# A transformer block on one core: gated channels tile by tile, keys' splits on VectorE, nearer deadlines in the planner

## The chip, the core and the metric

One core of a Trainium2 chip runs the whole kernel. The engines are TensorE (PE; its weight loads are listed as PEld), VectorE (DVE), ScalarE (ACT), GpSimd (POOL) and SyncE (SP, which issues the DMAs). The metric is the device time of one execution in microseconds (us); lower is better. Beside it stands a profile of one execution, with a time for each instruction.

## What is computed

One layer with batch 1, 1024 tokens, model width 1024 and 256 memory tokens, all in float32, in three residual sub-layers:

```python
h = rms_norm(x, pre_mix_g)
z = h @ w_in + b_in                         # 1024 x 1792
z_a, z_b, z_c = z[:, :256], z[:, 256:1024], z[:, 1024:]
y_a = pool_mixer(z_a, pool_w, pool_scale)   # trailing means over 2, 4, 8, 16 tokens, per-group linear
y_b = spatial_gating_mixer(z_b, ...)        # gelu, layer norm, 128x128 causal token mix, gate
y_c = conformer_conv_mixer(z_c, ...)        # a*sigmoid(g), 31-tap causal conv, layer norm, swish
x = x + rms_norm(concat([y_a, y_b, y_c]) @ w_out, post_mix_g)

h = rms_norm(x, pre_x_g); m = rms_norm(mem, mem_g)
x = x + rms_norm(cross_attention(h, m, wq, wk, wv, wo), post_x_g)   # 4 heads of 256

h = rms_norm(x, pre_ff_g)
x = x + rms_norm(square(relu(h @ w_ff1)) @ w_ff2, post_ff_g)        # width 4096
```

The part `z_c` is 768 wide: 384 values `a` and 384 gates `g`. The 384 gated channels are three tiles of 128.

## The kernel before

**Products.** Each float32 operand is split into a high part (`hi`, a rounded copy, made by ScalarE) and a low part (`lo`, the source less the high part, made by `lo_of` on VectorE or GpSimd). `mm3` (line 445) then makes three matmuls: hi x hi, hi x lo, lo x hi. The large square products (`om`, the mixer's output projection; `pq`, the queries; `ox`, the attention's output projection; and both MLP products `fx`, `fz`, `fy` and `g`) are made by `seven` and like helpers, with seven half-size products in place of eight and sums of operands on VectorE.

**Order by a planner.** The program is not issued as it is written. `Schedule.record` (line 148) notes every operation with its engine, its modelled cost (`_cost`, line 204), what it depends on, and its place in the record. `order` (line 231) then plans up to six times: each pass takes TensorE's order from the pass before (the first pass takes that of the record), and the pass with the shortest modelled span is issued. In `_order` (line 249) an operation gets a due time. It starts as TensorE's modelled time at that place of the record plus `SLACK`, 50000 ns, and is then lowered by those who use its result, down to the TensorE instruction that needs it:

```python
                due[i] = at + self.SLACK
...
                due[i] = min(due[i], due[u] - o.cost - self.LAT[op.eng][o.eng])
```

The planner places, again and again, the operation that can start first; among operations of an engine that can start at the same time, the nearer due time wins (on TensorE, the earlier place in the record). A PSUM bank (eight of 128x512, line 423) or a slot in SBUF is given when its first user is placed, as long as tiles recorded earlier can still get theirs. Each engine then runs its instructions in the order so found. A load on SP waits until TensorE has issued what was recorded 150 TensorE instructions before it.

**The first stage, up to `om`.** `norm_in` (line 558) normalises the tokens of one half (512 tokens, four blocks of 128), transposes them and leaves `h1[hf][k]` with both parts. The loop at line 602 makes the gated channels: for tile `j` and token half `hf`, 24 matmuls for the gates (`zg`), 24 for the values (`za`), a sigmoid on ScalarE (`sg`), and on VectorE the gated product into `hc[j]`, stored as even and odd tokens, and their sum into `hs[j]`. Its order is (0,0), (1,0), (0,1), (1,1), (2,0), (2,1). Within the first turn the second half of the tokens is normalised and tile 1's weights are loaded and split:

```python
            W("zc1")
            norm_in(1, [0, 1, 2, 3])
```

`conv_taps(j)` (line 644) needs all tokens of tile `j`: 47 scaled additions on VectorE in three sums, each in a PSUM bank (`cacca`, `caccb`, `caccc`), then the sum into `cs`. `conv_norm(hf, cs)` (line 666) transposes blocks of 128 tokens (`cnat`), takes mean and variance on VectorE, the reciprocal root on GpSimd (`rstd_of`, line 454: names ending in `e` are the request, in `r` the root), normalises on VectorE (`cn`), transposes back (`cback`) and applies gain, bias and swish (`csg`). It is recorded behind the keys but with a lead of 300 places (lines 869 to 872).

Beside this run the other mixers (`zb`, `sv`, `ybt`; pooling adds `zw` on GpSimd and `zp` on VectorE, line 727), the memory's normalisation (`memt`, `mT`) and the keys: `mem_product("wk")` (line 839) holds four PSUM banks (`wkp`) and takes 12 matmuls for each of eight rows of weights `wk0` to `wk7`; its result is copied (`kn`) and transposed (`kt`, `kT`). The rows of weights come from `row_unit` (line 504): a load of 128x1024, the high part on ScalarE, the low part either as one VectorE subtraction or as two GpSimd ones of 128x512. Line 519 chooses: rows of `w_in` (`ZR`) and of the keys (`WK`) on GpSimd, rows of the values (`WV`) on VectorE.

`om` starts with its first product, from channels 0 to 511 of the first half (`oma10`, `oma11`) and the first quarter of `w_out` (`omww10`, `omww11`); the convolution's channels come in with its second. Behind it follow the values (`wvp`), `pq`, attention, `ox` and the MLP.

Of the kernel before, what the change touches and what calls it, by code (L numbers as in the profile page):

```python
# [20 lines left out]
NK = D // P  # L21
# [44 lines left out]
class Schedule:  # L66
# [12 lines left out]
           "pe": {"act": 197, "dve": 196, "pe": 0, "pool": 200, "sync": 100},  # L79
           "pool": {"act": 75, "dve": 60, "pe": 309, "pool": 102, "sync": 100},  # L80
           "sync": {"act": 2100, "dve": 2100, "pe": 2100, "pool": 2100, "sync": 2100}}
    SLACK = 50000.0
    PASSES = 6
    BYDUE = ("act", "dve", "pool", "sync")
    TABLE = {AF.Sigmoid: "sigmoid", AF.Gelu_apprx_tanh: "gelu", AF.Exp: "exp"}
# [117 lines left out]
    @staticmethod  # L203
    def _cost(eng, method, args, kw, ins):
        n = 1
        for d in args[0].shape[1:]:
            n *= d
        if method == "dma_start":
            return max(450.0, n * args[0].shape[0] * 4 / 240.0)
        size = lambda a: int(np.prod(a.shape[1:]))  # L210
        if eng == "pe":
            passes = 4 if method == "matmul" and args[1].dtype == F32 else 1
            return max(109.0, 13.4 + passes * n * 0.4167)
        wide = [a for a in ins if size(a) > 1]
        ptrs = len(ins) - len(wide) if n > 1 else 0
        if eng == "act":
            c = 51.0 + 0.833 * n + (0.0 if ins[0].space == bass.MemoryType.PSUM else 42.0)
            return c + 93.0 * min(ptrs, 1) + (93.0 if "accum_out" in kw else 0.0)
        if eng == "pool":
            if method == "tensor_tensor":  # L220
                return 520.0 if n < 17 else 60 + 2.4 * n
            return 60 + 1.0 * n
        n = max([n] + [size(a) for a in wide])
        psum = any(a.space == bass.MemoryType.PSUM for a in ins + [args[0]])
        if not psum and len(wide) == 1 and method in ("tensor_scalar", "tensor_scalar_mul",
                                                      "tensor_copy"):
            return 69 + 0.52 * n + 61.0 * ptrs
        return 69 + 1.042 * n + 61.0 * ptrs
# [20 lines left out]
    def _order(self, pe_order):  # L249
# [18 lines left out]
        for i, op in enumerate(ops):  # L268
            if op.eng == "pe":
                at = max(at, due[i])  # L270
            else:
                due[i] = at + self.SLACK
        for i in range(len(ops) - 1, -1, -1):
# [129 lines left out]
def block_kernel(ctx: ExitStack, tc: tile.TileContext, x, mem, pre_mix_g, w_in, b_in, pool_w,  # L403
# [5 lines left out]
    act, dve, pool, pe, sync = sc.act, sc.dve, sc.pool, sc.pe, sc.sync  # L409
# [10 lines left out]
    def slot(name, shape, dt=F32):  # L420
        return sc.slot(name, shape, dt)

    def bank(name):
        return sc.tile(pp, [P, 512], F32, "b", 8, name)
# [91 lines left out]
            return hi, lo  # L516
        return go

    ZR, WK, WV = [pool] * NK, [pool] * NK, [dve] * NK
    units, made = {}, {}  # L520
    for j in range(3):
        units[f"zc{j}"] = col_unit(f"zc{j}", [(w_in, 1024 + j * P), (w_in, 1408 + j * P)], j == 0)
# [7 lines left out]
    def W(name):  # L530
        if name not in made:
            made[name] = units[name]()
        return made[name]
# [5 lines left out]
    def columns(name, vecs):  # L539

        rows = slot(name + "r", [P])
        at, res = 0, []
        n_all = sum(n for _, n in vecs)
        cols = sc.tile(cp, [P, n_all], F32, name, 1, name)
        for v, n in vecs:
            src = v if v.shape[0] == n else v.rearrange("o (r p) -> (o r) p", p=P)
            sync.dma_start(rows[at:at + n, :], src)
            res.append(cols[:, at:at + n])
            at += n
        ps = bank(name + "p")  # L550
        pe.transpose(ps[:, :n_all], rows[:n_all, :], ident[:n_all, :n_all])
        dve.tensor_copy(cols, ps[:, :n_all])
        return res
# [4 lines left out]
    def norm_in(hf, blocks):  # L558

        if h1[hf] is None:  # L560
            h1[hf] = [slot(f"h1_{hf}_{k}", [2, H], F32R) for k in range(NK)]
        nb = len(blocks)
        xs, ms = [], small(f"p0ms{hf}{blocks[0]}", 4)
        for b in blocks:
            bb = hf * 4 + b
            xt = slot(f"x{bb}", [D])
            sync.dma_start(xt, x[bb * P:(bb + 1) * P, :])
            act.activation(junk, xt, AF.Square, scale=1.0 / 32, accum_out=ms[:, b:b + 1])
            r = rstd_of(f"p0{bb}", ms[:, b:b + 1], 1)
            dve.tensor_scalar_mul(xt, xt, r)  # L570
            xs.append(xt)
        if not g:
            g.append(columns("gmix", [(pre_mix_g, 8)])[0])
            W("zc0")
        per = 4 // nb
        c = slice(blocks[0] * P, (blocks[-1] + 1) * P)
        for k0 in range(0, NK, per):
            bk = bank(f"p0t{hf}{blocks[0]}{k0}")
            for k in range(k0, k0 + per):
                ps = bk[:, (k - k0) * nb * P:(k - k0 + 1) * nb * P]  # L580
                for i in range(nb):
                    pe.transpose(ps[:, i * P:(i + 1) * P], xs[i][:, k * P:(k + 1) * P], ident)
            for k in range(k0, k0 + per):
                ps = bk[:, (k - k0) * nb * P:(k - k0 + 1) * nb * P]
                act.activation(h1[hf][k][:, 0, c], ps, AF.Identity, scale=g[0][:, k:k + 1])
                dve.scalar_tensor_tensor(h1[hf][k][:, 1, c], ps, g[0][:, k:k + 1],
                                         h1[hf][k][:, 0, c].bitcast(F32), ALU.mult, ALU.subtract)
# [5 lines left out]
    def prod_t(ps, w, a, b, act_h, c0=0, c1=H):  # L593
        for k in range(NK):
            mm3(ps[:, c0:c1], w[0](k, a, b), w[1](k, a, b), act_h[k][:, 0, c0:c1],
                act_h[k][:, 1, c0:c1], k == 0, k == NK - 1)
# [2 lines left out]

    hc = [slot(f"hc{j}", [2, H]) for j in range(3)]  # L600
    hs = [slot(f"hs{j}", [H]) for j in range(3)]
    for j, hf in ((0, 0), (1, 0), (0, 1), (1, 1), (2, 0), (2, 1)):
        w = W(f"zc{j}")
        pa, pg = bank(f"za{j}{hf}"), bank(f"zg{j}{hf}")
        if (j, hf) == (0, 0):
            for q in range(2):
                if q:
                    norm_in(0, [2, 3])
                prod_t(pg, w, 128, 256, h1[hf], q * 256, q * 256 + 256)
                prod_t(pa, w, 0, 128, h1[hf], q * 256, q * 256 + 256)  # L610
            W("zc1")
            norm_in(1, [0, 1, 2, 3])
            (g_x, g_ff, g_mem, bA, bC, pscale, cb, clg, clb, sgb) = columns("vec", [
                (pre_x_g, 8), (pre_ff_g, 8), (mem_g, 8), (b_in[:, 0:256], 2), (b_in[:, 1024:1792], 6),
                (pool_scale, 2), (conv_b, 3), (conv_ln_g, 3), (conv_ln_b, 3), (sg_b[0], 4)])
            cw = columns("taps", [(conv_w[0].rearrange("k (j p) -> (k j) p", p=P), 93)])[0].rearrange(
                "p (k j) -> p k j", j=3)
        else:
            prod_t(pg, w, 128, 256, h1[hf])
            prod_t(pa, w, 0, 128, h1[hf])  # L620
        sg = slot(f"sg{j}{hf}", [H])
        act.activation(sg, pg, AF.Sigmoid, bias=bC[:, 3 + j:4 + j])
        c = slice(hf * 256, hf * 256 + 256)
        dve.scalar_tensor_tensor(hc[j][:, :, c], pa.rearrange("p (n t) -> p t n", t=2),
                                 bC[:, j:j + 1], sg.rearrange("p (n t) -> p t n", t=2),
                                 ALU.add, ALU.mult)
        dve.tensor_tensor(hs[j][:, c], hc[j][:, 0, c], hc[j][:, 1, c], ALU.add)
# [703 lines left out]
    for ch in range(2):  # L1331
# [17 lines left out]
        for i, g, first in ((1, 0, True), (2, 1, True), (6, 0, False), (5, 1, True), (7, 0, False),  # L1349
# [22 lines left out]
            n = 1 if ch == 1 and i == 4 else 3  # L1372
# [60 lines left out]
```

## Time and profile before

| | |
|---|---|
| median of 3 runs | 1169.54 us (1169.51 to 1169.66) |
| the profiled execution | 1169.37 us |
| its span, first to last instruction | 1167.7 us |
| TensorE busy | 1142.2 us (98%) |
| VectorE busy | 917.0 us (79%) |
| ScalarE busy | 570.9 us (49%) |
| GpSimd busy | 168.2 us (14%) |
| granted TensorE clock, mean | 0.995 of full |

In all views times are us from the start of the span. Busy time of TensorE is modelled at its end, since matmuls overlap: a matmul of 512 columns is listed with some 390 ns and yet one follows the other every 227 ns. Nearly all rows have the line L162, where the planner's record calls the engine, so groups are told apart by the tiles' names: out<-in, buffer numbers partly left out. An idle time in brackets is followed by what ended it.

### The profile page before, as it was taken

The page shows a single profiled execution, that of the slowest core. Times are in us where ns is not written, and L with a number is a line of the kernel's source. Part 1 is how long each engine was busy: PE and PEld are TensorE (multiplying, and loading weights), DVE is VectorE, ACT ScalarE, POOL GpSimd, SP SyncE. Part 2 cuts the span into 40 slices and gives each one's busy share as a digit, 9 for nine tenths or more (in the row PEclk, how much of TensorE's full clock was granted, in tenths as well). Part 3 has the DMA queues.
Part 4 walks back from the last instruction along what each step waited for, and adds up shares of the span by engine and source line. Part 5 has one row for each costly group of instructions (what it writes and reads, how often), then busy time and mean ns, then how long its engine had stood idle before and what let it go on. Part 6 is the DMA issues. An engine that isn't in the chain of part 4 may idle for free.

```text
span 1167.7 us, 14569 instructions
## 1 busy us (share of the span) xinstructions
PE 1142.2 (98%) x5319; PEld 948.6 (81%) x5319; DVE 917.0 (79%) x1278; ACT 570.9 (49%) x998; POOL 168.2 (14%) x194
## 2 busy tenths in 40 slices
PE   7999999799999999999999999999999999999997
PEld 6788877688887898888888888888888888888885
DVE  5499999898988769988999777567679744487736
ACT  6332145666984368749843343334446433435321
POOL 4360229301347000013000000000000000000001
PEclk9999999899999999999999999999999999999999
DMA  7400025114761222236045535443775444443443
GB/s 263 146 30 1 1 89 207 47 62 150 256 253 55 90 72 91 73 119 225 17 136 210 186 137 184 158 146 116 241 263 189 162 163 155 153 160 116 174 144 145
DMA packets 87078, 163.11 MB, mean 140 GB/s; under 512 B 6474, under 2 KB 29918, under 8 KB 87006
## 3 DMA queue, kind: packets, MB, share of 16 engines
q1 hardware_dynamic: 87006, 162.17, 39.8%
q8 instruction: 42, 0.69, 0.2%
q14 instruction: 30, 0.25, 0.1%
HBM read 116.01 MB, written 46.14 MB: 139 GB/s over the span
## 4 chain that ended last, share of the span: by engine, by line
PE 87%; DVE 7%; ACT 4%; issue 1%; POOL 0%; DMA 0%; POOLq 0%; DVEq 0%; ACTq 0%
PE g L162 25%; PE fx L162 13%; PE fz L162 7%; PE om L162 7%; PE pq L162 6%; PE ox L162 5%; PE zb L162 4%; PE fy L162 3%; PE zg L162 3%; PE za L162 3%; PE sc L162 2%; PE o L162 2%; PE wvp L162 2%; PE wkp L162 2%; DVE caccc L162 1%; ACT oxh L162 1%
## 5 line engine op out<-in xcount | busy, mean ns | idle before, releaser
L162 POOL TENSOR_TENSOR fr0r<-fr0e,half 128x1 f32<-128x1 f32 x1 | 0.9, 863 | 581.9 <-DVE fr0e L162 581.9
L162 ACT COPY c<-fx 128x512 f32<-128x512 f32 x48 | 29.0, 603 | 87.8 <-PE fx L162 84.6
L162 DVE TENSOR_TENSOR acc<-acc,g 128x512 f32<-128x512 f32 x40 | 26.9, 684 | 46.1 <-PE g L162 46.1
L162 DVE TENSOR_TENSOR c<-c,fz 128x512 f32<-128x512 f32 x32 | 22.0, 687 | 16.5 <-ACT c L162 16.5
L162 DVE SCALAR_TENSOR_TENSOR c<-c 128x512 f32<-128x512 f32 x48 | 33.3, 693 | 0.7
L162 DVE SCALAR_TENSOR_TENSOR caccc<-hs,cws,caccc 128x511 f32<-128x511 f32 (+14 forms) x45 | 33.5, 744 | 0.2
L162 DVE SCALAR_TENSOR_TENSOR cacca<-hc,taps,cacca 128x511 f32<-128x511 f32 (+14 forms) x45 | 32.2, 746 | 0.0
L162 ACT ACTIVATE junk<-acc 128x512 f32<-128x512 f32 x16 | 10.2, 635 | 44.7 <-DVE acc L162 42.7
L162 DVE TENSOR_TENSOR w1o<-w1a,w1o 128x512 fp32r<-128x512 f32 x32 | 21.6, 689 | 12.6 <-ACT w1o L162 12.6
L162 DVE SCALAR_TENSOR_TENSOR caccb<-hc,taps,caccb 128x511 f32<-128x511 f32 (+13 forms) x42 | 30.5, 745 | 0.0
L162 PE MATMUL sc<-kv,q 128*128 128x256 f32 x192 | 27.5, 288 | 0.0
L162 ACT CAST w1o<-w1a 128x512 fp32r<-128x512 f32 x32 | 19.6, 640 | 14.7 <-DVE sb L162 6.2
L162 PEld LDWEIGHTS sc<-kv,q 128*128 128x128 f32 x192 | 24.9, 190 | 0.7
L162 DVE TENSOR_TENSOR sa<-c 128x512 f32<-128x512 f32 x16 | 11.1, 695 | 18.0 <-ACT c L162 16.5
L162 ACT ACTIVATE c<-fx 128x512 f32<-128x512 f32 x16 | 9.6, 598 | 31.6 <-PE fx L162 31.6
L162 PE MATMUL o<-pT,kv 128*128 128x512 f32 x96 | 24.4, 393 | 0.0
L162 ACT CAST w1o<-w1c 128x512 fp32r<-128x512 f32 x32 | 19.5, 624 | 6.9 <-PE fx L162 4.1
L162 PE MATMUL fx<-h3a10h,w1o 128*128 128x512 f32 x64 | 22.7, 392 | 0.0
L162 DVE TENSOR_TENSOR w1o<-w1c,w1o 128x512 fp32r<-128x512 f32 x32 | 21.6, 689 | 1.2 <-ACT w1o L162 1.2
L162 PE MATMUL fx<-h3a60h,w1o 128*128 128x512 f32 x64 | 22.5, 389 | 0.0
L162 PE MATMUL fx<-h3a11h,w1o 128*128 128x512 f32 x64 | 22.3, 389 | 0.0
L162 PE MATMUL fx<-h3a70h,w1o 128*128 128x512 f32 x64 | 22.3, 389 | 0.0
(1656 smaller groups left out, 4116.8 us busy)
## 6 DMA issues: line engine op xcount, KB each, us to landing
ha<-scr_hid SPq DMA_DIRECT2D x56, 512.0 KB
scr_hid<-c SPq DMA_DIRECT2D x48, 256.0 KB
scr_hid<-sa SPq DMA_DIRECT2D x32, 256.0 KB
scr_hid<-sb SPq DMA_DIRECT2D x32, 256.0 KB
x<-in_x_dram SPq DMA_DIRECT2D x8, 512.0 KB
omwb<-in_w_out_dram SPq DMA_DIRECT2D x8, 512.0 KB
omx<-in_x_dram SPq DMA_DIRECT2D x8, 512.0 KB
scr_x<-omx SPq DMA_DIRECT2D x8, 512.0 KB
```

The costliest lines, as they stand in the source:

```text
L162: op.fn = lambda: f(*[put(a) for a in args], **{k: put(v) for k, v in kw.items()})
```

## The change

Four edits. `SLACK` goes from 50000 to 20000 ns, so that work whose result TensorE does not need soon falls due 30 us earlier. The modelled rate of a DMA goes from 240 to 270 bytes per ns, in the planner only. The low parts of the keys' weights are made by VectorE, one subtraction of 128x1024 for each of the eight rows, instead of by GpSimd in two halves. And the gated channels are recorded with both token halves of tile 0 first, then both of tile 1, then both of tile 2; where weights are fetched and the second half of the tokens is normalised is recorded as before.

```diff
-    SLACK = 50000.0
+    SLACK = 20000.0
...
-            return max(450.0, n * args[0].shape[0] * 4 / 240.0)
+            return max(450.0, n * args[0].shape[0] * 4 / 270.0)
...
-    ZR, WK, WV = [pool] * NK, [pool] * NK, [dve] * NK
+    ZR, WK, WV = [pool] * NK, [dve] * NK, [dve] * NK
...
-    for j, hf in ((0, 0), (1, 0), (0, 1), (1, 1), (2, 0), (2, 1)):
+    for j, hf in ((0, 0), (0, 1), (1, 0), (1, 1), (2, 0), (2, 1)):
         w = W(f"zc{j}")
```

## Rows read from the trace of the kernel before

**Rows 1.** The page's first part: busy time (share of the span) and instructions.

```profile
span 1167.7 us, 14569 instructions
...
PE 1142.2 (98%) x5319; PEld 948.6 (81%) x5319; DVE 917.0 (79%) x1278; ACT 570.9 (49%) x998; POOL 168.2 (14%) x194
```

**Rows 2.** Busy time by stretch, later stages. Columns: stretch, its us, engines, clock, DMA.

```profile
313.00:337.00 24.00, 24.00 (x124) 20.28 (x123) 22.32 (x25) 18.72 (x52) 9.35 (x8) 1.00 0.74 257
...
545.00:582.00 37.00, 36.83 (x178) 30.08 (x176) 36.14 (x45) 32.92 (x73) 5.92 (x6) 1.00 0.19 66
...
860.00:1150.00 290.00, 290.00 (x1281) 240.23 (x1280) 191.05 (x196) 116.21 (x140) 4.03 (x5) 1.00 0.46 161
```

**Rows 3.** The same view, first stage up to the output projection.

```profile
44.00:55.00 11.00, 11.00 (x50) 9.13 (x49) 1.94 (x4) 1.62 (x2) 2.52 (x2) 1.00 0.16 49
...
98.00:140.00 42.00, 41.44 (x192) 34.09 (x191) 41.94 (x82) 10.31 (x23) 6.69 (x9) 1.00 0.00 1
...
140.00:190.00 50.00, 48.49 (x230) 38.81 (x229) 48.63 (x95) 22.68 (x39) 21.69 (x25) 1.00 0.35 122
...
200.00:219.00 19.00, 18.57 (x93) 14.44 (x93) 16.02 (x26) 6.99 (x11) 12.18 (x11) 1.00 0.38 139
...
219.00:232.00 13.00, 7.51 (x38) 5.49 (x37) 10.96 (x24) 12.63 (x24) 3.69 (x4) 0.74 0.00 1
```

**Rows 4.** Timeline of TensorE: start us, us, what, xcount, [idle before <-releaser].

```profile
18.04 1.91 PE L162 MATMUL p0t<-ident,x 128*128 128x128 f32 x16
...
31.71 0.73 PE L162 MATMUL zg<-h,zc1h 128*128 128x512 f32 x2
...
43.25 0.61 PE L162 MATMUL zg<-h,zc0h 128*128 128x512 f32 x2
...
191.57 0.49 PE L162 MATMUL cnat<-ident,cs 128*128 128x128 f32 x3
...
219.02 0.60 PE L162 MATMUL cback<-ident,cn 128*128 128x128 f32 x4
...
231.36 0.69 PE L162 MATMUL om<-omww10h,oma10h 128*128 128x512 f32 x1
```

**Rows 5.** Timeline of VectorE, same columns.

```profile
29.59 5.36 DVE L162 SCALAR_TENSOR_TENSOR h<-p0t,gmix,h 128x512 fp32r<-128x512 f32 x8 [1.14 <-ACT h L162]
...
55.53 0.75 DVE L162 TENSOR_SCALAR cacca<-hc,taps 128x512 f32<-128x512 f32 x1
...
57.49 0.75 DVE L162 TENSOR_SCALAR caccc<-hs,cws 128x512 f32<-128x512 f32 x1
...
188.36 0.74 DVE L162 SCALAR_TENSOR_TENSOR cs<-caccc,cb,cua 128x512 f32<-128x512 f32 x1
...
213.45 1.22 DVE L162 TENSOR_TENSOR oma11l<-yq,oma11h 128x1024 fp32r<-128x1024 f32 x1
...
214.58 0.67 DVE L162 TENSOR_SCALAR cn<-cnat,cmv,cr00r 128x384 f32<-128x384 f32 x1
```

**Rows 6.** Timelines of VectorE, then GpSimd: the root's request, a split, the root.

```profile
193.23 0.15 DVE L162 TENSOR_SCALAR cr00e<-cmv 128x1 f32<-128x1 f32 x1
...
204.23 3.41 POOL L162 TENSOR_TENSOR wk7l<-wk7r,wk7h 128x512 fp32r<-128x512 f32 x2
...
207.60 0.99 POOL L162 TENSOR_TENSOR cr00r<-cr00e,half 128x1 f32<-128x1 f32 x1
```

**Rows 7.** Groups by line and shape, VectorE, 44:232 (xcount | busy us, mean ns | idle).

```profile
L162 DVE SCALAR_TENSOR_TENSOR zp<-zw,zaT 64x512 f32<-64x512 f32 x4 | 6.1, 1532 | 0.1
...
L162 DVE SCALAR_TENSOR_TENSOR zp<-zw,zaT 64x496 f32<-64x496 f32 x4 | 2.7, 667 | 0.1
...
L162 DVE TENSOR_TENSOR oma10l<-yq,oma10h 128x1024 fp32r<-128x1024 f32 x1 | 2.4, 2355 | 0.0
...
L162 DVE TENSOR_TENSOR omww10l<-omwb,omww10h 128x1024 fp32r<-128x1024 f32 x1 | 1.2, 1226 | 0.0
```

**Rows 8.** Waits of TensorE, whole span (us in total, times, longest).

```profile
PE pq L162 <- DVE h2a61l L162: 0.9, 1, 0.9
```

## The prediction

> **What bounds the kernel now.** I read the page first: TensorE works 1142.2 of 1167.7 us [rows 1]. The change removes no TensorE work, so what it can win is TensorE's lost time. I then cut the span into stretches. From 860 us on nothing is lost: TensorE is busy 290 of 290 us with VectorE at 191 [rows 2]. In 313:337 and 545:582 TensorE is also full, but VectorE is nearly so (22.32 of 24, 36.14 of 37): places where order can hurt. The large loss lies just ahead of the output projection of the mixer. In 219:232 TensorE works 7.51 of 13 us and its granted clock averages 0.74 [rows 3]; the clock fell behind idle time, toward the lower of its two levels (1.2 of 2.4 GHz), and so stretches the work that is left.
>
> The size of that hole: from the transpose at 219.02 to the first `om` matmul at 231.36 are 12.3 us [rows 4]. Of the 38 instructions in 219:232 [rows 3], three are matmuls and 35 are transposes. Sixteen transposes in a row took 1.91 us with the last one's end, so one costs about 0.11 us and 35 cost 3.8. **The hole is 8.5 us**; the stretch before it, 200:219, loses 0.4.
>
> Why it is there: `om`'s first product was not late. Its last operand, `oma11l`, is written at 213.45, for 1.22 us [rows 5]. What is left for the end is the normalisation of the convolution (`cnat`, `cback`) and `kt`. The first `cnat` comes at 191.57 [rows 4], after the last convolution sum at 188.36 [rows 5]; but the reciprocal root of its variance, asked for by VectorE at 193.23, is made by GpSimd only at 207.60 [rows 6]. GpSimd's queue was in the keys' weight splits, 3.4 us for the last of eight alone [rows 6]. For 14 us each `cnat` keeps its PSUM bank, beside the four banks of the keys' product, out of eight. The whole normalisation is so pushed behind that product, and at the end runs as a bare chain ScalarE, VectorE, TensorE.
>
> **The order of channels.** It moves 48 matmuls and their sigmoid and products; DMAs are recorded where they were. Before, tile 1's first half runs from 31.71 to 43.25 and tile 0's second half follows [rows 4]; the first tap is at 55.53 [rows 5]. After, tile 0 is whole when TensorE reaches 43.25, and taps start about 10.5 us sooner. VectorE worked only 1.94 of the 11 us in 44:55 [rows 3], so **9.1 us of idle VectorE time are filled**. From 98 to 190 it is full (41.94 of 42, 48.63 of 50), so this moves its whole queue forward. What it costs on TensorE: tile 0's second half needs the second token half normalised, which tile 1's first half did not. VectorE writes those eight `h` low parts from 29.59 over 5.36 us [rows 5], so the last is there at 34.95; TensorE, starting at 31.71 and using at least three matmuls of 0.23 us for each, wants the last at 36.5. I take 0; if it waited for all of them, +3.2; if weights of tile 1 that come late stop mattering, -0.5. On the queues, tile 1's splits (GpSimd) and loads (SP) only gain 11 us of time.
>
> **Keys' splits on VectorE.** Removed from GpSimd: 16 halves, 3.4 us for the pair shown. Added on VectorE: eight of 128x1024. The same form starts at 213.45 and its successor at 214.58 [rows 5], so 1.13 us each, **9.1 us**, in the stretch where VectorE is full. Behind each wait the taps and then the keys' product, which takes 12 matmuls (2.7 us) for each split. That alone would eat the head start. Against it stands time that VectorE loses to GpSimd now: `oma10l` took 2355 ns where `omww10l`, the same form, took 1226; `zp` of 64x512 took 1532 where 64x496 took 667 [rows 7]. That is 1.1 and four times 0.8: about 4.5 us that come back, if no other GpSimd work takes the place. The pooling adds stay on GpSimd; if each of the eight new splits ran into one and lost 1.1 us as `oma10l` did, 8.8 us would be paid again. Bounds of this term: -5.5 and +4.3 (8.8 less 4.5). I take -4.5, since the pooling adds are a short burst and the splits are spread over the loads. VectorE's balance up to 219 is -9.1 + 9.1 - 4.5 = **-4.5 us**, and the 14 us wait for the root [rows 6] goes, whatever the balance.
>
> The Trainium skill (SBUF — State Buffer, "Who interferes with whom") says that a VectorE instruction with two SBUF inputs and a GpSimd one that reads SBUF exclude each other for a whole instruction. By that rule, the trace agrees: `oma10l`, with two inputs in SBUF, took twice its time. The rule also speaks against the move, since the new splits have two SBUF inputs as well: by it the 8.8 us would be paid, and the sum would be the first rival's smaller price.
>
> **Nearer deadlines, and the modelled DMA rate.** `SLACK` and the 270 of `_cost` issue nothing; they alter the planner's order on ScalarE, VectorE, GpSimd and SP, and so, through its passes, TensorE's. Work that has no TensorE user soon (pooled channels, evictions that are parked, residual and hidden stores) comes 30 us sooner in line. Ahead of 232 us that pulls pooling before taps: neutral. Behind it, in the stretches with VectorE full [rows 2], it can put parked values before the split that TensorE is about to need. There the only wait above 0.3 us now is 0.9 for `h2a61l` [rows 8]. I take 0: the cover is TensorE's own full work. If that cover is gone, each misplaced 128x1024 operation costs 1.1 to 2.4 us [rows 7]; bounds for all: -1 and +4.
>
> **The sum.** The normalisation then runs beside the keys' product, and `om` starts when that ends. I keep 1.5 us of the hole for the last copies and `kt` (what is late next are the four copies of the keys on ScalarE, which free the banks), near the loss of the stretch before it rather than that of the hole. -8.5 + 1.5 = -7.0; the 0.4 of 200:219 goes too; head 0; deadlines 0. The profiled execution, 1169.37 us, gives 1169.37 - 7.4 = **1162.0 us**. (It stands 0.17 under the median of 1169.54, which changes nothing.) With the ends: -10 (the whole hole, the 0.4, 1 more) gives 1159; keeping 5 us of the hole and paying 2 in order gives 1167.
>
> **Rivals.**
> *VectorE's queue gets longer, not shorter* (slower). Place: 98 to 190, where it is full; price: each us of a positive balance moves the last convolution sum, and with it the end of the hole, by a us, once the 14 us of the root no longer give way; it decides where the first `cnat` starts later than 191.57. The balance turns positive in two ways. Eight splits held up by pooling adds: +4.3, 1169.4 + 4.3 = 1174. Or a head start of nothing: taps need PSUM banks, and the gate products hold four while they run; if tile 0's sums don't get three at 44, the 9.1 us of splits stand alone: 1178. For it: VectorE is full from 98 on [rows 3]. Against it: three sums got banks between 55.53 and 57.49 [rows 5], while gate products ran. Chance 0.13.
> *The hole moves* (no change). In 219:232 ScalarE is busy 12.63 of 13 us [rows 3]: 24 instructions, those of the normalisation, the key copies and splits of `omww`. If they still bunch at the end, because the banks and not GpSimd set it, only 1 to 2 us come: 1168. For it: the four copies of the keys. Against: ScalarE is at 6.99 of 19 just before, free to take them sooner. Chance 0.14.
> *Deadlines cost what the hole gives.* Two or three misplaced splits in the full stretches, 4 to 6 us back: 1166 to 1168. Chance 0.09.
> *The order is not followed.* The planner picks by readiness; if tile 1's first half is still taken first at 31.7, the head start is gone but the root is quick: half the hole, 1166, or nothing. Chance 0.04.
>
> **How the numbers follow.** A measurement of this kernel can tell about 0.2%, 2.3 us, from no change: faster is below 1167.2, slower above 1171.9. The forecast has 0.60 (1159 to 1167). The third and fourth rival fall about half under 1167.2. So faster 0.67, same 0.18, slower 0.15 (the first rival, and a little for an order that is bad everywhere). The range takes the forecast, the second to fourth rival, and the lower bounds: 1157 to 1172.
>
> **What would show it.** In the changed profile: the first tap near 45 us; VectorE over 8 of 11 us in 44:55; GpSimd with no keys' splits, and a root within 1 us of its request; `zp` of 64x512 near 0.7 us; first `cnat` by 188; the first `om` matmul near 224 with the clock at full in the 10 us before; everything behind it the same distance from `om` as now. I am wrong if `cnat` comes after 191.6, if a hole of over 4 us stands ahead of `om`, or if TensorE loses time after 232 that it did not lose before.

## The result, and the profile after

The changed kernel takes 1158.41 us (median; 1158.23 to 1158.74) against 1169.60 of the kernel before on the same chip. The ratio is 0.9902, 95% interval [0.9885, 0.9919]: **faster by 11.2 us**, within the range of 1157 to 1172 and 3.6 us below the forecast of 1162.

The page's first lines and the clock of its slices, to set beside [rows 1]:

```profile
span 1156.9 us, 14603 instructions
...
PE 1138.7 (98%) x5319; PEld 946.6 (82%) x5319; DVE 924.8 (80%) x1286; ACT 571.6 (49%) x998; POOL 151.9 (13%) x178
...
PEclk9999999999999999999999999999999999999999
```

VectorE has eight instructions more, GpSimd sixteen fewer: the keys' splits. The same stretches as in [rows 3] (stretch, its us, busy us of PE, PEld, DVE, ACT, POOL, granted clock, DMA):

```profile
44.00:55.00 11.00, 11.00 (x50) 9.09 (x50) 11.00 (x18) 1.63 (x2) 2.73 (x3) 1.00 0.07 27
...
98.00:140.00 42.00, 42.00 (x195) 34.76 (x194) 41.69 (x82) 9.57 (x21) 8.11 (x12) 1.00 0.00 1
140.00:190.00 50.00, 48.98 (x232) 39.09 (x231) 46.73 (x95) 25.47 (x43) 11.81 (x15) 1.00 0.40 135
...
200.00:219.00 19.00, 18.76 (x94) 14.37 (x92) 18.36 (x36) 13.83 (x25) 3.36 (x5) 1.00 0.45 159
219.00:232.00 13.00, 12.71 (x65) 10.60 (x65) 12.07 (x19) 11.84 (x21) 0.91 (x2) 1.00 0.00 1
```

VectorE is busy in all of 44:55, where it had 1.94 us. In 219:232 TensorE works 12.71 us where it had 7.51, and the granted clock stays at 1.00, where the stretch with idle time averaged 0.74. The hole is gone. TensorE's timeline around it, beside [rows 4]:

```profile
188.24 0.49 PE L162 MATMUL cnat<-ident,cs 128*128 128x128 f32 x3
...
217.90 0.39 PE L162 MATMUL wkp<-wk7h,mT 128*128 128x512 f32 x1
218.13 0.38 PE L162 MATMUL kt<-ident,kn 128*128 128x128 f32 x2
218.75 0.80 PE L162 MATMUL kt<-ident,kn 128*128 128x128 f32 x2 [0.24 <-ACT kn L162]
219.69 0.50 PE L162 MATMUL om<-omww10h,oma10h 128*128 128x512 f32 x1
```

`om` starts at 219.69 instead of 231.36. Of these 11.7 us about 2 are only moved: 18 transposes (12 `kt`, 6 `cback`) now run after `om` has begun, where none did. VectorE and GpSimd, beside [rows 5, 6]:

```profile
43.72 0.74 DVE L162 TENSOR_SCALAR cacca<-hc,taps 128x512 f32<-128x512 f32 x1
...
170.32 1.39 DVE L162 SCALAR_TENSOR_TENSOR cs<-caccc,cb,cua 128x512 f32<-128x512 f32 x2
...
190.24 0.15 DVE L162 TENSOR_SCALAR cr00e<-cmv 128x1 f32<-128x1 f32 x1
...
206.17 1.22 DVE L162 TENSOR_TENSOR oma11l<-yq,oma11h 128x1024 fp32r<-128x1024 f32 x1
```

```profile
191.09 0.86 POOL L162 TENSOR_TENSOR cr00r<-cr00e,half 128x1 f32<-128x1 f32 x1
```

The taps start 11.8 us sooner, the last convolution sum comes 17 us sooner, and the root follows its request after 0.9 us instead of 14.4. And the forms of [rows 7] at their new length (groups by line and shape, 44:232):

```profile
L162 DVE SCALAR_TENSOR_TENSOR zp<-zw,zaT 64x512 f32<-64x512 f32 x4 | 2.7, 684 | 0.1
...
L162 DVE TENSOR_TENSOR oma10l<-yq,oma10h 128x1024 fp32r<-128x1024 f32 x1 | 1.2, 1224 | 0.6 <-PE zb L162 0.6
...
L162 DVE TENSOR_TENSOR wk0l<-wk0r,wk0h 128x1024 fp32r<-128x1024 f32 x1 | 1.2, 1207 | 0.0
```

`zp` and `oma10l` are no longer stretched: 4 x 0.85 + 1.1 = 4.5 us came back on VectorE. The split of `wk0` is one of the eight that VectorE now makes.

**Where the 10.8 us of span came from.** The first `pq` matmul moved from 336.89 to 328.21, so 8.7 us were won by then. The hole gave about 7.4 of them: 8.5 lost us became 1.1, counted from the last matmul of the keys' product (217.90) to `om` (219.69), less that matmul and the transposes between. The waits at the memory's transposes (184 to 189) gave some 1.6; the rest evens out. Behind it, attention's first product moved by 9.83, so `pq` gave another 1.1: the wait for `h2a61l` [rows 8] is gone. The last 1 us came in the MLP.

### The profile page after: what moved, and what is told of

It reads as the page before. It is cut to its first block, busy times and chain, and to the rows that moved or that the text cites. A ratio compares the mean times of both kernels' runs of the same rounds, so it can differ in the third digit from the quotient of the medians.

```text
span 1156.9 us, 14603 instructions
## 1 busy us (share of the span) xinstructions
PE 1138.7 (98%) x5319; PEld 946.6 (82%) x5319; DVE 924.8 (80%) x1286; ACT 571.6 (49%) x998; POOL 151.9 (13%) x178
## 4 chain that ended last, share of the span: by engine, by line
PE 94%; DVE 2%; ACT 2%; issue 1%; POOL 0%; DMA 0%; POOLq 0%; DVEq 0%; ACTq 0%
PE g L162 25%; PE fx L162 15%; PE zb L162 8%; PE fz L162 8%; PE ox L162 7%; PE pq L162 7%; PE om L162 6%; PE fy L162 4%; PE zg L162 3%; PE za L162 3%; PE sc L162 2%; PE o L162 2%; PE wvp L162 2%; PE pT L162 1%; PE wkp L162 0%
## 5 line engine op out<-in xcount | busy, mean ns | idle before, releaser
L162 PE MATMUL fz<-h3a51h,w1o 128*128 128x512 f32 x64 | 22.3, 389 | 0.0
L162 PE MATMUL fy<-h3a20h,w1o 128*128 128x512 f32 x64 | 22.3, 389 | 0.0
L162 PE MATMUL fy<-h3a21h,w1o 128*128 128x512 f32 x64 | 22.3, 389 | 0.0
```

Source lines behind the costliest of these rows:

```text
L162: op.fn = lambda: f(*[put(a) for a in args], **{k: put(v) for k, v in kw.items()})
```

## The experiments

Every run was timed beside the kernel before on its own chip. The ratio is that to it; the us are the ratio's distance from 1 times 1170. The last four columns are read from each profile: start of the first `om` matmul, wait from the first block's request (`cr00e`) to its root (`cr00r`), start of the last convolution sum, and the hole, counted as the prediction counts it: from the start of the keys' product's last matmul to `om`, less 0.227 us for that matmul and 0.109 for each transpose between (in e9 the keys' product ends behind `om`). The profiles of e2, e4, e9 and e10 are of executions 2.6 to 9.3 us above their medians.

| run | edits of the change in it | ratio [95%] | us | om | root | sum | hole |
|---|---|---|---|---|---|---|---|
| before | none | 1 | 0 | 231.4 | 14.4 | 188.4 | 8.5 |
| changed | order, keys, SLACK, rate | 0.9902 [0.9885, 0.9919] | -11.5 | 219.7 | 0.9 | 171.0 | 1.1 |
| e1 | order | 1.0016 [1.0007, 1.0025] | +1.9 | 231.7 | 13.8 | 169.6 | 7.2 |
| e2 | keys | 1.0014 [1.0005, 1.0024] | +1.6 | 227.3 | 1.1 | 191.8 | 0.3 |
| e3 | SLACK | 0.9979 [0.9970, 0.9989] | -2.5 | 228.9 | 14.7 | 187.6 | 7.1 |
| e4 | rate | 1.0031 [1.0005, 1.0057] | +3.6 | 237.3 | 8.7 | 184.5 | 8.5 |
| e5 | order, keys | 0.9954 [0.9937, 0.9970] | -5.4 | 224.5 | 0.2 | 170.2 | 0.3 |
| e6 | order, keys, SLACK | 0.9956 [0.9941, 0.9971] | -5.1 | 227.7 | 0.2 | 171.0 | 1.9 |
| e7 | order, keys, rate | 0.9934 [0.9920, 0.9949] | -7.7 | 225.6 | 0.3 | 169.7 | 0.4 |
| e8 | order, SLACK, rate | 0.9987 [0.9978, 0.9997] | -1.5 | 232.3 | 12.2 | 168.5 | 8.2 |
| e9 | changed, GpSimd splits too | 1.0015 [1.0006, 1.0024] | +1.8 | 230.2 | 0.2 | 168.5 | - |
| e10 | changed, keys' splits twice | 0.9985 [0.9976, 0.9995] | -1.8 | 223.9 | 0.3 | 173.2 | 1.0 |
| e11 | keys, SLACK, rate | 0.9958 [0.9943, 0.9973] | -4.9 | 221.8 | 0.6 | 189.7 | 0.3 |
| e12 | changed, SLACK 10000 | 0.9929 [0.9915, 0.9944] | -8.3 | 221.4 | 0.9 | 171.2 | 1.0 |

**Each edit alone.** e1, the order:

```diff
-    for j, hf in ((0, 0), (1, 0), (0, 1), (1, 1), (2, 0), (2, 1)):
+    for j, hf in ((0, 0), (0, 1), (1, 0), (1, 1), (2, 0), (2, 1)):
```

> The kernel before with the order of the gated channels alone. Main theory (VectorE's head start and GpSimd's queue each make part of the hole): taps start near 44 us and the last convolution sum comes some 9 us earlier, but the root still waits behind the keys' splits on GpSimd, so only 3 to 5 us come: about 1165 us. Rival 'VectorE's queue alone': the whole gain, 1159. Rival 'GpSimd's queue alone': 1168 to 1170. Rival 'nearer deadlines': no change, 1169.

e2, the keys:

```diff
-    ZR, WK, WV = [pool] * NK, [pool] * NK, [dve] * NK
+    ZR, WK, WV = [pool] * NK, [dve] * NK, [dve] * NK
```

> The kernel before with the keys' low parts on VectorE alone. Main theory: VectorE's queue grows by 9.1 less the 4.5 us that it no longer loses to GpSimd, the first cnat comes some 4 us later, but the root comes at once: about 1165 to 1167 us. Rival 'VectorE's queue alone': slower, about 1174. Rival 'GpSimd's queue alone': nearly the whole gain, 1160 to 1162. Rival 'nearer deadlines': no change.

Both numbers were missed: I expected a part of the gain from each, and neither gave any. The profiles say why. In e1 the convolution is done at 169.6, and still (timelines of VectorE, GpSimd and TensorE):

```profile
195.78 0.14 DVE L162 TENSOR_SCALAR cr00e<-cmv 128x1 f32<-128x1 f32 x1
```
```profile
206.21 3.42 POOL L162 TENSOR_TENSOR wk7l<-wk7r,wk7h 128x512 fp32r<-128x512 f32 x2
209.59 1.53 POOL L162 TENSOR_TENSOR cr00r<-cr00e,half 128x1 f32<-128x1 f32 x1
```
```profile
231.72 0.78 PE L162 MATMUL om<-omww10h,oma10h 128*128 128x512 f32 x1
```

The root waits for the last key split as before, and `om` starts where it did. In e2 the root comes at once, but TensorE waits at other places, for VectorE and ScalarE. Its timeline at the start of `om`, then its waits (us in total, times, longest):

```profile
225.03 0.39 PE L162 MATMUL wkp<-wk7h,mT 128*128 128x512 f32 x1
225.26 2.29 PE L162 MATMUL kt<-ident,kn 128*128 128x128 f32 x16
227.31 0.47 PE L162 MATMUL om<-omww10h,oma10h 128*128 128x512 f32 x1
```

```profile
PE om L162 <- DVE kT L162: 3.1, 1, 3.1
...
PE zat L162 <- ACT zaT L162: 1.6, 1, 1.6
PE memt L162 <- ACT zaT L162: 1.6, 1, 1.6
PE om L162 <- DVE oma60l L162: 1.3, 1, 1.3
```

The hole ahead of `om` is down to 0.3 us there, and the loss stands behind: TensorE is idle for 6.2 us between `om` (227.31) and 313, where the kernel before had none behind its `om`, and its granted clock averages 0.96 in that stretch. Half of it is the wait for `kT`, for which the hole before had 3.9 us of waits. So moving the keys' splits clears the way to `om` without the head start, and VectorE's longer queue gives the time back behind it. The order alone leaves 7.2 us of the hole.

The last column of the table says the same of all runs: 7.1 to 8.5 us in the five kernels with the keys' splits on GpSimd alone, 0.3 to 1.9 in all others that have the column.

e3 and e4, the planner's numbers (`SLACK` 20000; 270 in `_cost`):

> The kernel before with SLACK 20000 alone. Main theory: neither of the two queues is relieved, the hole of 219:232 stays: 1168 to 1171 us. Rival 'nearer deadlines': half of the gain or more, 1158 to 1164.

> The kernel before with the modelled DMA rate of 270 alone. Main theory: no change beyond the planner's scatter, 1168.5 to 1170.5 us; no DMA is issued differently and TensorE waits for none after the first us. A rival in which loads issued in another order matter: over 2 us either way.

e3 came out at 1167.51 us, 0.5 below the range expected; the hole is there (`om` at 228.9). e4 was expected to change nothing and is slower, in an odd way: seven of its ten runs took 1169.70 to 1171.68 us and three 1180.71 to 1181.10. Its +3.6 us hangs on the three; the other seven stand 0.9 us above the median of the kernel before, 1170.03. The last section shows what happened in one of the three.

**The pair, and the change without one edit each.**

> The kernel before with the order of the channels and the keys' low parts on VectorE, and nothing else. Theory now: the hole ends when the later of two queues is done, GpSimd's root and VectorE's splits; either edit alone leaves the other queue, the pair relieves both, so nearly the whole gain comes: 1158 to 1162 us, with the root within 2 us of its request and the last convolution sum near 171. Rival 'the planner's scatter' (the gain is that of one lucky order): no gain for the pair, 1166 to 1172.

> The changed kernel with the keys' low parts back on GpSimd. Two-queue theory: the root waits again for GpSimd's splits (over 8 us), the hole of 6 us or more is back ahead of the output projection: 1167 to 1171 us. Rival 'VectorE's head start is what counts': 1158 to 1161.

e5 shows that the two belong together: +1.9 and +1.6 alone, -5.4 as a pair, with the root 0.2 us behind its request. From e1 to e5 the keys take the hole from 7.2 to 0.3 us; from e2 to e5 the order takes TensorE's idle time between `om` and 313 from 6.2 to 3.0. But its 1165.08 us is not the 1158 to 1162 expected; half of the gain is missing. e8 came out as expected (1168.84): with the keys on GpSimd the root waits 12.2 us and `om` starts at 232.3, although VectorE has its head start and the planner its new numbers.

> The changed kernel with the old order of the channels. Two-queue theory: GpSimd is relieved, VectorE is not (last convolution sum past 188), so little or nothing comes: 1166 to 1172 us. Rival 'GpSimd's queue alone, the rest being scatter': 1158 to 1163.

e11, 1165.22 us, lies between the theories. Its hole is gone (0.3) and `om` starts at 221.8, but VectorE is late behind it: TensorE works 78.38 us of 232:313, where the kernel before had all 81.00. The head start is thus worth 6.6 us in the full change. Of the 6.0 us by which the two profiles' spans differ, 2.2 stand ahead of `om`, 2.8 between it and the first `pq` matmul, and 1.1 behind that.

> The changed kernel with the modelled DMA rate back at 240. Two-queue theory: both queues stay relieved, 1157 to 1161 us. Rival 'the planner's scatter': anything up to 1169.

> The changed kernel with SLACK back at 50000. Two-queue theory: 1158 to 1162 us, some 0 to 2 us above the changed kernel, since SLACK alone gave 2 us. Rival 'nearer deadlines make the gain together with the order': 1165 to 1170.

Both planner numbers matter once the pair is there: without the rate 6.4 us are missing, without `SLACK` 3.8. e7, 1162.35 us, missed its range by 0.35, and its reasons too (0 to 2 us were expected to be missing); e6 missed. Part of what is missing is a wait that the order itself brings. In e1 and e5 to e9 it costs 3.1 us (in the stretch 140:190 TensorE is idle for 3.1 to 4.0 us, where the kernel before had 1.5), in e10 1.8; the changed kernel and e12 keep 1.0 of it. First e7 on TensorE and VectorE, then the changed kernel:

```profile
145.93 1.57 PE L162 MATMUL sv<-vv,swt 128*128 128x192 f32 x8 [1.70 <-DVE vv L162]
148.22 0.41 PE L162 MATMUL ybt<-ident,zz 128*128 128x128 f32 x2 [0.72 <-DVE zz L162]
```
```profile
144.09 0.61 DVE L162 SCALAR_TENSOR_TENSOR zz<-zz,vmv,sgn 128x384 f32<-128x384 f32 x1
```
```profile
143.47 1.46 PE L162 MATMUL sv<-vv,swt 128*128 128x192 f32 x8
```
```profile
141.13 0.61 DVE L162 SCALAR_TENSOR_TENSOR zz<-zz,vmv,sgn 128x384 f32<-128x384 f32 x1
```

Once taps are ready early, they crowd out the gating mixer's `zz` and `vv`, for which TensorE has nothing else to do; the changed plan puts those two 3 us sooner, ahead of four taps. Neither number alone does it: e6 has the nearer deadlines and e7 the new rate, and both wait. From e5 to the changed kernel TensorE's idle time in 140:190 falls from 3.1 to 1.0 us and that between `om` and 313 from 3.0 to 0.5: 4.6 of the 6.1 us that the two numbers give there.

e12 asked whether still nearer deadlines give still more:

> The changed kernel with SLACK 10000. If nearer deadlines pull the gating mixer's steps ahead of the taps, and that is what SLACK gave, a nearer one still gives up to 2 us more (the waits at 144 to 147): 1156 to 1158 us. Rival 'SLACK only draws another order': 1158 to 1164.

They do not: 1161.63 us. The waits near 145 are as in the changed kernel, and new ones open in the MLP's first product:

```profile
PE fx L162 <- DVE h3a71l L162: 1.2, 1, 1.2
PE fx L162 <- DVE h3a70l L162: 1.1, 1, 1.1
PE fx L162 <- ACT c L162: 0.7, 1, 0.7
```

So on these three values `SLACK` draws another order rather than working as a dial.

**Loading each queue again.** In both, the low parts of the keys are made an extra time, over the same place: in e9 by GpSimd first, in e10 by VectorE.

```diff
             if eng is dve:
+                if name[:2] == "wk":
+                    for c in (slice(0, D // 2), slice(D // 2, D)):
+                        lo_of(pool, lo[:, c], raw[:, c], hi[:, c])
                 lo_of(dve, lo, raw, hi)
```
```diff
             if eng is dve:
+                if name[:2] == "wk":
+                    lo_of(dve, lo, raw, hi)
                 lo_of(dve, lo, raw, hi)
```

> The changed kernel, in which GpSimd makes the keys' low parts as before (16 halves) and VectorE then makes them once more over the same place. VectorE has the queue of the changed kernel and GpSimd that of the kernel before. If GpSimd's queue holds the hole: the root waits over 6 us again, om starts past 227 and the time is 1166 to 1172 us. Rival 'only VectorE's load and the planner's order count': the root's wait may come back, but the time stays at 1158 to 1162.

> The changed kernel with each of the keys' eight low parts made twice on VectorE: 9.1 us more in VectorE's queue between 176 and 203, GpSimd as in the changed kernel. In the changed kernel the operands of om's first product are ready 12 us before it, so if VectorE has room again: 1158 to 1161 us. Rival 'VectorE is still what sets the start of om': all 9 us come back, 1166 to 1168.

e9's time, 1171.78 us, fell where GpSimd's queue was to put it, but not by that path: the root waits 0.2 us. What became late is the keys' product (last matmul at 234.6, in the changed kernel 217.9), whose rows now pass two engines. It settles nothing about the root. e10 went the rival's way: 1168.12 us, 9.7 more than the changed kernel, for 9.1 us of VectorE work. `om` starts at 223.9, 4 us late; the rest comes behind it, where TensorE is idle for 3.6 us of 232:300 and its granted clock averages 0.95. Its waits:

```profile
PE om0t L162 <- DVE omt L162: 1.9, 1, 1.9
...
PE om L162 <- DVE oma60l L162: 0.8, 1, 0.8
PE om1t L162 <- DVE omt L162: 0.8, 1, 0.8
```

**VectorE has little room.** In the changed kernel the operands of `om`'s first product are ready 12 us early, but that is the planned order and no reserve: in e10 their last split, `oma11l`, comes 17.7 us later (at 223.85), and VectorE is busy 62.5 of the 68 us of 232:300 (61.1 in the changed kernel).

## Why the prediction was right, and where its sum was not

**Right: the hole, its size and its end.** 8.5 us were lost there, 1.5 were to stay, 1.1 stayed. The steps named for the profile came: first tap near 45 (43.7), VectorE full in 44:55, the root within 1 us (0.9), `zp` at 0.7 (0.684), the first `cnat` by 188 (188.24), the clock at full ahead of `om`. Two steps did not: `om` starts at 219.7, not near 224, and `pq` follows it after 108.5 us, not 105.5 (2 of the 3 are the moved transposes). Of the signs of being wrong one came, but small: TensorE loses 0.5 us of 232:313, where it had lost none. The 4.5 us lost to GpSimd came back as priced. That the hole ahead of `om` goes with the keys' splits on GpSimd is shown by all kernels that have the column. The first rival's price is real, too: e10 pays about a us for each us of VectorE work. It did not decide because the head start was there; without it e2 is slower, and e11 6.6 us short.

**Wrong: VectorE's queue as one sum that also sets the end of the hole.** Of "each us of a positive balance moves the last convolution sum, and with it the end of the hole, by a us", the first half nearly held in e2: with a balance of 9.1 - 4.5 = +4.6 the sum came 3.4 us later. The second half failed there: the hole ahead of `om` shrank to 0.3, and the price was paid behind it. With a head start neither held: the order alone moved that sum by 19 us, not by 9.1, since other work fell in behind the taps, and most of the hole stayed (7.2); in e1, e5 and the changed kernel the sum comes at 169.6 to 171.0. The rival's 1178 also leaves out the 4.5 us that come back: by the prediction's own terms a head start of nothing gives 1174, and e2 measured +1.6. And the sign I named for slower, a first `cnat` after 191.6, failed: it came at 192.4 in e7 and 192.5 in e6, and both are faster than the kernel before.

**Wrong: "ahead of 232 us ... neutral" and "I take 0"** for the planner's numbers. The pair gave 5.4 us, where 7.4 had been summed for the mechanism, and the two numbers together gave another 6, where 0 stood, with bounds of -1 and +4. That term was mis-sized and its lower bound too near: bounds of -6 would have been needed. The order also has a cost that I did not price, the gating mixer crowded out by taps (2.4 us of waits at 146 and 148 in e7), and the splits have one behind `om` (3.0 us of idle TensorE in e5). The planner's numbers took most of both away again. With these errors of both signs the sum was 3.6 us too cautious; that it came so near is in part luck, since two costs and the gain that covers them all stood at nothing.

**Wrong in the first expectations:** half of the gain for each edit. Moving the keys' splits ends the hole ahead of `om` (8.5 to 0.3 in e2); the order takes little of it (8.5 to 7.2 in e1) and pays for what the splits cost elsewhere.

**Open.** That the root's wait itself holds the hole is not shown apart from the rest of GpSimd's splits. All five kernels with the keys on GpSimd alone (before, e1, e3, e4, e8) have a wait of 8.7 to 14.7 us and `om` at 228.9 or later, all others at most 1.1 us, with `om` at 230.2 (e9), 227.7 or earlier; the one run that was to separate it (e9) did not. The root on another engine was not tried. Nor does the root alone set the pace in the kernel before: it is there at 208.59, and the first `cn` runs only at 214.58 [rows 5, 6], behind splits that the plan put first (in e1 7.6 us behind its root, in e8 9.3; in the changed kernel 1.4). The plan also never lets a GpSimd `tensor_tensor` (a split, a pooling add, a root) overlap a VectorE operation with two inputs in SBUF (`port` in `_order`), so moving the splits changes what it can place; no run tells that from GpSimd's queue on the chip. Why rate and `SLACK` need each other is not settled either, and the two without the pair were not run: six plans are made and the best by the model is taken, so a small step in a constant can pick another plan. No run beat the changed kernel.

## What to carry to other kernels

An experiment with one edit can show nothing, or a loss, although the edit did what it was to do: in e2 the hole ahead of `om` was gone and the loss stood behind it. Look in the profile, place by place, for what it gave and what it cost before dropping it; another edit may pay the cost. Before moving work to an engine, read how full it is in the stage behind, not only where the work lands. And with a planner, the effect of a constant has to be measured with the edits that it goes with: here the same constant gave +3.6 us alone (+0.9 without the three long runs) and -6.4 in company.

## What the runs showed of the hardware that I had not expected

A VectorE instruction can be held for far longer than one GpSimd instruction. In e4's profile one such instruction with two inputs in SBUF (`zz`, `sgn`), 0.61 us elsewhere, takes 11.81 us; GpSimd started its first pooling add 0.04 us after it and ran ten instructions without a gap, each within 0.06 us of what the same forms take undisturbed in the kernel before (1.06 to 1.30). Timelines of VectorE and GpSimd:

```profile
189.12 11.81 DVE L162 SCALAR_TENSOR_TENSOR zz<-zz,vmv,sgn 128x384 f32<-128x384 f32 x1
200.85 0.47 DVE L162 SCALAR_TENSOR_TENSOR mT<-memt,vec,mT 128x256 fp32r<-128x256 f32 x1
```
```profile
189.16 2.13 POOL L162 TENSOR_TENSOR zw<-zaT 128x527 f32<-128x527 f32 x2
191.21 1.10 POOL L162 TENSOR_TENSOR zw<-zw 128x525 f32<-128x525 f32 x1
192.23 1.33 POOL L162 TENSOR_TENSOR wk5l<-wk5r,wk5h 128x512 fp32r<-128x512 f32 x1
...
199.21 1.31 POOL L162 TENSOR_TENSOR wk6l<-wk6r,wk6h 128x512 fp32r<-128x512 f32 x1
```

VectorE goes on when GpSimd's train ends. That the train caused it is read from this one profile; no run varied it. TensorE runs dry 9 us after it started and waits 6.9 us for the result; its granted clock averages 0.70 in 200:206. The Trainium skill (SBUF — State Buffer, "Who interferes with whom") has the two engines exclude each other, whoever issues first holding what they share for its whole instruction; here the instruction that is listed first was held, over ten of the other's, and the measurement decides. I had priced such a meeting at 1.1 us; this one cost 11.2. The same program took 1180.71 to 1181.10 us in three runs of ten and 1169.70 to 1171.68 in seven; the profile is of one of the three, so that the seven lack the long block is an inference from their times. In the same stretch of the changed kernel the longest extra time of a VectorE instruction is 0.7 us, and no split of GpSimd's stands beside it.
